# Weight parts split at a layer's end, on VectorE alone, and a layer that begins with the products of upper parts

## The chip, the cores and the metric

The kernel runs on one core of one Trainium2 chip. The metric is the device time of one execution in microseconds (us), from three runs of the kernel before: 2188.71, 2190.86 and 2193.92, median 2190.86. A separate execution was profiled; the rows in this document come from it.

Five engines run side by side, each in the order of its own instruction list, and wait for each other through semaphores: TensorE (PE, and PEld for its weight loads), VectorE (DVE), ScalarE (ACT), GpSimd (POOL) and SyncE (SP), which issues the large loads.

## The reference

The kernel computes two blocks in a row for 256 tokens of 1024 features. Block 1 (attention and 64 experts) takes the first half of the span and is not touched. Block 2 has two layers, each with a feed-forward part, a mixer and a second feed-forward part; every one of these six parts ends in a layer norm whose output is all that the next part reads:

```python
def swiglu(x, w_gate, w_up, w_down):
    return (jax.nn.silu(x @ w_gate) * (x @ w_up)) @ w_down

def second_block(x, mem, ln_g, ln_b, ...):
    alpha = DEEPNORM_ALPHA
    for l in range(DEPTH_2):                       # 2 layers
        x = layer_norm(alpha * x + 0.5 * swiglu(x, ffn_w_gate[l, 0], ffn_w_up[l, 0], ffn_w_down[l, 0]),
                       ln_g[l, 0], ln_b[l, 0])
        mem_kv = mem @ w_kv_mem[l]
        if l % N_MIXERS == 0:
            u = x @ w_in_conv[j]                   # convolution mixer
            tok = short_conv_mixer(u[..., :3 * D_TOK], conv_w[j])
        else:
            u = x @ w_in_mlstm[j]                  # mLSTM mixer
            tok = mlstm_mixer(...)
        xa = memory_cross_attention(u[..., -D_XA:], mem_kv)
        mix = jnp.concatenate([tok, xa], -1) @ w_out[l]
        x = layer_norm(alpha * x + mix, ln_g[l, 1], ln_b[l, 1])
        x = layer_norm(alpha * x + 0.5 * swiglu(x, ffn_w_gate[l, 1], ffn_w_up[l, 1], ffn_w_down[l, 1]),
                       ln_g[l, 2], ln_b[l, 2])
    return x
```

All weights and activations are float32, and the feed-forward width is 2816.

## The kernel before

**Products of two parts.** A float32 product is made of three faster ones. Each weight w is split into an upper part wh (a rounded copy, `wh`, made by ScalarE) and a lower part wl = w - wh (a subtraction); the activations likewise, as the pair of tiles `xT`. Then x @ w is taken as xh·wh + xh·wl + xl·wh, three matmuls into one PSUM bank (`mm3`, called by `xw`, L1144). A weight part is 1 MB: a load into one of the three raw slots of the ring (`wc` or `wr`, set by L1753), the copy wh on ScalarE, the subtraction wl on VectorE, or on GpSimd where `split` (L1100) is called with gp=True. The raw slot is free again after the subtraction. The two parts go to one of six pairs of tiles, taken in turn (four pairs from the mLSTM mixer on); a pair is free when the last matmul has read it.

**Blocks of tokens.** The 256 tokens are two blocks of 128, b = 0 and b = 1. At the end of a part of block 2 the sum of block 0 is finished first, three units of 12 matmuls before that of block 1 (the list at L1309, and the one in `mix_out`, L1368). Then `lnorm` (L1155) normalises the block: VectorE adds the residual (`h<-h,fd` or `h<-h,mo`), takes statistics, a few Newton steps on a column (L156 to L165), and two passes over each half (L1183, L1184); TensorE transposes each half (`lt`), ScalarE and VectorE make the two parts of `xT` from it. Nothing of the next part can be multiplied for a block until its `xT` is there.

**A part's beginning.** `ffn` (L1212) takes its width in chunks of 256 and five times 512. It begins with three weight tiles: the gate's and the up-projection's columns of the first chunk (`g0`, `u0`), and two halves of the second chunk's gate (`g1`), L1276 onward: all products of block 0 with g0, u0 and both halves of g1, then the same for block 1. g0 and both halves of g1 are split on GpSimd. The convolution mixer begins with three parts too (two on GpSimd or ScalarE and VectorE in turn), then a fourth on GpSimd; the mLSTM mixer with four on GpSimd, and one part of its w_out is also split there. The subtractions on VectorE are put by the scheduler behind the latest norm (`issue_after(self.after[1])`), unless marked early.

**What sets the order.** TensorE's order is the order of the program: large products are units, and the short steps of the norms and of other dependent chains go between them when the program's own clock says they are due, or when `wait` asks for their result. The other engines' order comes from a scheduler. SP's loads are in program order, each waiting for its raw slot.

Of the kernel before, what the change touches and what calls it, by code (L numbers as in the profile page):

```python
# [10 lines left out]
F32 = mybir.dt.float32  # L11
# [14 lines left out]
LN_EPS = 1e-5  # L26

# [45 lines left out]
class MixT:  # L73
    """Eight tiles of features in two places: the first n, and the others."""
# [13 lines left out]
class Kern:  # L88
# [29 lines left out]
    def slot(self, shape, name, pool=None):  # L118
        """One 8 KB slot of the weight ring."""
# [22 lines left out]
    def rms(self, pool, st, eps, name):  # L142
        """(mean of squares + eps) ^ -0.5 from the statistics of two halves."""
# [9 lines left out]
    def rsqrt(self, pool, out, hx, name):  # L153
        """(2 hx) ^ -0.5 of a few columns: a first guess from the bits, then Newton steps."""
# [83 lines left out]
    # ---------------------------------------------------------------- block 1: attention  # L238
    def phase_a(self):
# [41 lines left out]
        # u = rmsnorm(h) * gain, transposed, columns [meta | x]  # L281
# [33 lines left out]
        # z, features on partitions  # L315
# [20 lines left out]
        def gates():  # L336
            """log_a: log_sigmoid(a_low @ w_a2 + b_a), the 1/16 sits in the triangle; and its sums in a chunk."""
# [35 lines left out]
        def wide(n, src, scale, name):  # L373
            """(src * scale + eps) ^ -0.5 of a wide tile: exp(-ln/2) and a Newton step."""
# [9 lines left out]
        def keys():  # L384
            """MLA: the keys and values, and the rope of the shared keys, doubled on the partitions."""
# [31 lines left out]
        def queries():  # L417
            """MLA: the queries, and their rope, a pair of heads on the partitions, the other one zeroed."""
# [1412 lines left out]
```

## Time and profile before

| what | value |
|---|---|
| median of three runs (lowest, highest) | 2190.86 us (2188.71, 2193.92) |
| span of the profiled execution, first to last instruction (the page gives no other time of it) | 2193.5 us |
| mean granted TensorE clock of that execution | 0.974 of full speed |
| PE busy | 2009.8 us, 92% of the span |
| DVE busy | 956.9 us, 44% |
| ACT busy | 669.1 us, 31% |
| POOL busy | 123.4 us, 6%, 49 instructions |

Block 2 runs from about 1151 us to the end. A slice of the page in which PE shows 8 instead of 9 contains the passage from one part of block 2 to the next; PEclk is 9 (over 90% of full speed) in nearly all of them. The span is a sum of long stretches in which TensorE never waits and of six passages in which it does: from block 1 into the first feed-forward part (about 1151 us), into the convolution mixer (1357), the second (1454) and the third (1649) feed-forward part, the mLSTM mixer (1841) and the fourth feed-forward part (1960 to 2000).

### The profile page before, as it was taken

How to read it: one execution, taken by the hardware profiler on the slowest of the kernel's cores; microseconds unless marked ns; L12 is line 12 of the kernel's file. 1: busy time of each engine (PE TensorE's matmuls, PEld its weight loads, DVE VectorE, ACT ScalarE, POOL GpSimd, SP SyncE). 2: the span in 40 equal slices, each digit the busy share in tenths (PEclk: the TensorE clock that was granted, in tenths of full speed). 3: DMA queues.
4: the chain of work that ended last, by engine and by line, in shares of the span. 5: the costliest groups of instructions: out<-in, count | busy, mean ns of one | idle time of the engine just before them, and what ended most of it. 6: DMA issues, size and time to landing. Idle time of an engine off the chain costs nothing. (4 is left out here: it accounts for less than half of the span.)

```text
span 2193.5 us, 36714 instructions
## 1 busy us (share of the span) xinstructions
PE 2009.8 (92%) x15959; PEld 1407.1 (64%) x15959; DVE 956.9 (44%) x1439; ACT 669.1 (31%) x885; POOL 123.4 (6%) x49
## 2 busy tenths in 40 slices
PE   8989898988888898888888999999999999998998
PEld 7777453534444353535457887878887887887886
DVE  6553322222222222222236445765447445787455
ACT  6422111111111111111124433544334432843432
POOL 4000000000000000000011002020010002012000
PEclk9979999999999999999998999999999999999999
DMA  6458999999999999999996554546555543435552
GB/s 223 173 190 348 402 397 411 413 411 412 413 413 412 412 413 411 412 408 413 402 350 217 186 178 153 180 155 214 182 173 193 191 165 101 156 138 173 190 175 76
DMA packets 195943, 604.97 MB, mean 276 GB/s; under 512 B 9889, under 2 KB 26529, under 8 KB 195778
## 3 DMA queue, kind: packets, MB, share of 16 engines
q1 hardware_dynamic: 195554, 602.55, 72.4%
q8 instruction: 127, 2.08, 0.4%
q14 instruction: 38, 0.31, 0.0%
q10 hardware_dynamic: 224, 0.03, 0.0%
HBM read 601.49 MB, written 1.05 MB: 275 GB/s over the span
## 5 line engine op out<-in xcount | busy, mean ns | idle before, releaser
L975 DVE SCALAR_TENSOR_TENSOR h<-po,G,h 128x512 f32<-128x512 f32 x256 | 192.2, 751 | 366.4 <-PE po L116 346.1
L116 PE MATMUL pd<-ed,hT 128*32 128x512 f32 x1024 | 251.4, 644 | 47.3 <-DMA ed<-in_expert_w_down 36.8
L1118 DVE TENSOR_TENSOR wl<-wc,wh 128x2048 fp32r<-128x2048 f32 (+1 forms) x94 | 213.3, 2270 | 168.1 <-ACT wh L1114 168.0
L1114 ACT ACTIVATE wh<-wc 128x2048 fp32r<-128x2048 f32 (+2 forms) x114 | 212.8, 1871 | 239.6 <-PE fu L116 76.4
L116 PE MATMUL fg<-wh,xT 128*128 128x512 f32 (+1 forms) x768 | 234.4, 382 | 8.0 <-DVE xT L1124 8.0
L116 PE MATMUL po<-y,C 128*128 128x512 f32 x512 | 236.7, 605 | 3.8 <-ACT C L969 3.8
L116 PE MATMUL fd<-wh,hT 128*128 128x512 f32 x704 | 235.3, 402 | 0.0
L116 PE MATMUL fu<-wh,xT 128*128 128x512 f32 (+1 forms) x768 | 229.2, 377 | 0.0
L116 PEld LDWEIGHTS po<-y,C 128*128 128x128 f32 x512 | 91.8, 189 | 144.6 <-ACT y L964 72.6
L1118 POOL TENSOR_TENSOR wl<-wc,wh 128x2048 fp32r<-128x2048 f32 (+2 forms) x20 | 87.2, 4367 | 1669.6 <-PE po L116 1012.5
L1118 DVE TENSOR_TENSOR wl<-wr,wh 128x2048 fp32r<-128x2048 f32 x51 | 116.9, 2292 | 130.7 <-ACT wh L1114 130.7
L116 PE MATMUL pu<-eu,xg 128*32 128x128 f32 x4096 | 131.7, 274 | 41.2 <-DMA eu<-in_expert_w_up 40.7
L116 PEld LDWEIGHTS fg<-wh,xT 128*128 128x128 f32 x768 | 142.3, 191 | 37.6 <-DVE xT L1124 9.1
L116 PEld LDWEIGHTS fu<-wh,xT 128*128 128x128 f32 x768 | 140.8, 188 | 28.9
L949 DVE TENSOR_TENSOR hg<-sg,pu 128x128 f32<-128x128 f32 x64 | 18.5, 289 | 308.9 <-PE pu L116 308.9
L116 PEld LDWEIGHTS fd<-wh,hT 128*128 128x128 f32 x704 | 132.9, 189 | 30.8
L116 PEld LDWEIGHTS pd<-ed,hT 128*32 128x32 f32 x1024 | 51.2, 114 | 152.9 <-issue 97.9
L116 PEld LDWEIGHTS pu<-eu,xg 128*32 128x32 f32 x4096 | 109.8, 110 | 56.1 <-DMA eu<-in_expert_w_up 44.4
L116 PE MATMUL fg<-wl,xT 128*128 128x512 f32 (+1 forms) x384 | 145.6, 379 | 0.0
L116 PE MATMUL fu<-wl,xT 128*128 128x512 f32 (+1 forms) x384 | 144.6, 377 | 0.0
L116 PE MATMUL fd<-wl,hT 128*128 128x512 f32 x352 | 139.3, 396 | 0.0
L969 ACT COPY C<-pc 128x256 f32<-128x256 f32 x64 | 23.9, 373 | 371.0 <-PE pc L113 371.0
(497 smaller groups left out, 2545.9 us busy)
## 6 DMA issues: line engine op xcount, KB each, us to landing
eg<-in_expert_w_gate SPq DMA_DIRECT2D x128, 1024.0 KB, 18.4
eu<-in_expert_w_up SPq DMA_DIRECT2D x128, 1024.0 KB, 18.4
ed<-in_expert_w_down SPq DMA_DIRECT2D x128, 1024.0 KB, 18.4
wc<-in_ffn_w_gate SPq DMA_DIRECT2D x44, 1024.0 KB, 4.9
wc<-in_ffn_w_up SPq DMA_DIRECT2D x44, 1024.0 KB, 4.9
wr<-in_ffn_w_down SPq DMA_DIRECT2D x44, 1024.0 KB, 4.7
wc<-in_w_in_conv SPq DMA_DIRECT2D x10, 1024.0 KB, 5.0
wr<-in_w_out SPq DMA_DIRECT2D x8, 1024.0 KB, 4.8
```

The lines of the kernel that those rows point to most:

```text
L116: self.nc.tensor.matmul(out, lhsT, rhs, start=start, stop=stop, **kw)
L949: nc.vector.tensor_mul(hg, sg, pu[:, :P])
L969: nc.scalar.copy(C, p[:, :NX])
L975: nc.vector.scalar_tensor_tensor(self.h[:, b, cs], p, self.G[:, b, e:e + 1], self.h[:, b, cs], ALU.mult, ALU.add)
L1114: nc.scalar.activation(hi, raw, AF.Copy)
L1118: (nc.gpsimd if gp else nc.vector).tensor_sub(lo, raw, hi.bitcast(F32))
```

## The change

Seven edits, all in block 2.

- No subtraction of a weight part runs on GpSimd; the 21 that did are given to VectorE.
- The first three weight parts of a part of block 2 are loaded and split at the end of the part before it, just after that part's last weight has been split (`nxt()` in `ffn` and `mix_out`); for the mLSTM mixer these are its first two, kept out of the two pairs that close before it (keep).
- These subtractions are marked early (not behind a norm), except at the first and the last feed-forward part (defer=True), where only wh is made at first and the subtraction is made by `lower`, behind the norm of both blocks.
- `xw` takes a list of passes. A feed-forward part begins with the passes UPPER (xh·wh and xl·wh) of the three parts for block 0, then for block 1, then with LOWER (xh·wl) for block 0 and for block 1; the second half of g1 follows whole.
- The convolution mixer begins in the same way with its three parts.
- The flags that put some of these copies and subtractions late are dropped.
- Comments are removed.

```diff
+ALL, UPPER, LOWER = (0, 1, 2), (0, 2), (1,)
-    def split(self, raw, gp=False, late=False, early=False):
+    def split(self, raw, gp=False, late=False, early=False, keep=False, defer=False):
...
-            pool = self.pairs.pop(0)
+            pool = self.pairs.pop(next(a for a, x in enumerate(self.pairs) if not keep or x not in self.brief))
...
+        if defer:
+            return hi, lo, raw
...
+    def lower(self, w):
+
+        if len(w) == 3:
+            with self.tc.issue_after(self.after[1].ins):
+                self.nc.vector.tensor_sub(w[1], w[2], w[0].bitcast(F32))
+        return w[:2]
...
+    def xw(self, b, out, w, k0, passes=ALL):
...
-                x = [t[:, b, k] for t in self.xT]
-                self.mm3(out, x, (hi[:, k - k0, :], lo[:, k - k0, :]), k == 0, k == KD - 1)
-        self.unit(3 * kk * n / 2380, go)
+                xh, xl = (t[:, b, k] for t in self.xT)
+                for q in passes:
+                    x, y = ((xh, hi), (xh, lo), (xl, hi))[q]
+                    self.mm(out, x, y[:, k - k0, :], start=k == 0 and q == 0,
+                            stop=k == KD - 1 and q == passes[-1] and passes != UPPER)
+        self.unit(len(passes) * kk * n / 2380, go)
...
+    def ffn_first(self, l, j, defer=False):
+
+        wg, wu = (self.i[n][l, j] for n in ("ffn_w_gate_2", "ffn_w_up_2"))
+        src = [self.cols_w(wg, 0, 256)[0], self.cols_w(wu, 0, 256)[0], self.cols_w(wg, 256, 512)[0]]
+        return [self.split(x(), early=True, defer=defer) for x in src]
+
+    def conv_first(self):
+        w = self.i["w_in_conv_2"]
+        return [self.split(self.cols_w(w, 512 * c, 512)[h](), early=True) for c, h in ((4, 0), (4, 1), (3, 0))]
+
+    def mlstm_first(self):
+        w = self.i["w_in_mlstm_2"]
+        return [self.split(x(), early=True, keep=True) for x in self.cols_w(w, 3072, 264)]
...
-        g0 = self.split(self.cols_w(wg, *chunks[0])[0](), True)
-        u0 = self.split(self.cols_w(wu, *chunks[0])[0](), l + j == 0, early=True)
-        gl = self.cols_w(wg, *chunks[1])
-        g1 = [self.split(gl[0](), True)]
-        gu(0, "g", 0, 0, g0)
-        g1.append(self.split(gl[1](), True, l + j == 0))
-        gu(0, "u", 0, 0, u0)
-        for h in range(2):
-            gu(1, "g", h, 0, g1[h])
-        gu(0, "g", 0, 1, g0)
-        gu(0, "u", 0, 1, u0)
-        for h in range(2):
-            gu(1, "g", h, 1, g1[h])
+        lead = [(0, "g", 0), (0, "u", 0), (1, "g", 0)]
+        ws = self.first
+        for b in range(2):
+            for (c, which, h), w in zip(lead, ws):
+                gu(c, which, h, b, w, UPPER)
+        ws = [self.lower(w) for w in ws]
+        for b in range(2):
+            for (c, which, h), w in zip(lead, ws):
+                gu(c, which, h, b, w, LOWER)
+        w = self.split(self.cols_w(wg, *chunks[1])[1]())
+        for b in range(2):
+            gu(1, "g", 1, b, w)
...
                 w[q] = self.split(ws[q]())
+                if q == 3 and nxt:
+                    self.first = nxt()
...
-                w[part] = self.split(parts[part](), l == 1 and part == 2)
+                w[part] = self.split(parts[part]())
+                if part == 1:
+                    self.first = nxt()
...
-        ws = {}
-        for c, h in ((4, 0), (4, 1), (3, 0)):
-            ws[c, h] = self.split(self.cols_w(w, 512 * c, 512)[h](), h == 0, early=True)
-        for c, h, b in [(4, 0, 0), (4, 1, 0), (3, 0, 0), (3, 1, 0), (4, 0, 1), (4, 1, 1), (3, 0, 1), (3, 1, 1)] + \
-                [(c, h, b) for c in (2, 1) for h in range(2) for b in range(2)] + \
+        ws = dict(zip(((4, 0), (4, 1), (3, 0)), self.first))
+        for b in range(2):
+            for (c, h), x in list(ws.items()):
+                part(c, h, b, x, UPPER)
+        for b in range(2):
+            for (c, h), x in list(ws.items()):
+                part(c, h, b, x, LOWER)
+        for c, h, b in [(3, 1, 0), (3, 1, 1)] + [(c, h, b) for c in (2, 1) for h in range(2) for b in range(2)] + \
                 [(0, 0, 0), (0, 1, 0), (0, 0, 1), (0, 1, 1)]:
             if (c, h) not in ws:
-                ws[c, h] = self.split(self.cols_w(w, 512 * c, 512)[h](), (c, h) == (3, 1))
+                ws[c, h] = self.split(self.cols_w(w, 512 * c, 512)[h]())
...
-            ws[G[0], h] = self.split(self.cols_w(w, *G)[h](), True)
+            ws[G[0], h] = self.first[h]
...
-        part(*Q[0], 0, 0, True)
-        p0 = part(*Q[0], 1, 0, True)
+        part(*Q[0], 0, 0)
+        p0 = part(*Q[0], 1, 0)
...
+                self.brief = [self.pair(more) for _ in range(2)]
+                self.first = self.ffn_first(0, 0, defer=True)
+                self.ffn(0, 0, 0, lambda: self.conv_first())
+                self.conv_mixer(0, lambda: self.ffn_first(0, 1))
+                self.ffn(0, 1, 2, lambda: self.ffn_first(1, 0))
+                self.ffn(1, 0, 0, lambda: self.mlstm_first())
+            self.brief = []
+            self.mlstm_mixer(1, lambda: self.ffn_first(1, 1, defer=True))
+            self.ffn(1, 1, 2, None)
```

Where it moves instructions, by the order of the built programs. **First, TensorE at the beginning of the second feed-forward part**, around the transposes `lt` of block 1's norm. xT_9588 and xT_9589 are the upper and lower part of the activations, `fu` the up-projection's and `fg` the gate's products. Before, they stand behind all 24 products of g0 and all 24 of u0 for block 0 and are followed by those of g1 for block 0:

```order
L116 MATMUL fu_11717<-wh_11674,xT_9588 128x256
L116 MATMUL fu_11717<-wl_11675,xT_9588 128x256
L116 MATMUL fu_11717<-wh_11674,xT_9589 128x256
L113 MATMUL lt_11742<-cst_63,h 128x128 x4
L116 MATMUL fg_11753<-wh_11680,xT_9588 128x512
L116 MATMUL fg_11753<-wl_11681,xT_9588 128x512
L116 MATMUL fg_11753<-wh_11680,xT_9589 128x512
```

Now:

```order
L117 MATMUL fg_11718<-wh_11564,xT_9588 128x512
L117 MATMUL fg_11718<-wh_11564,xT_9589 128x512
L114 MATMUL lt_11727<-cst_63,h 128x128 x4
L114 MATMUL lt_11734<-cst_63,h 128x128 x4
L117 MATMUL fg_11741<-wh_11552,xT_9588 128x256
L117 MATMUL fg_11741<-wh_11552,xT_9589 128x256
```

Ahead of these transposes now stand 40 products of block 0: 16 of g0, 16 of u0 (256 columns each) and 8 of the first half of g1 (512 columns); before, 48 of 256 columns, with 24 of 512 to follow before block 1's. Behind them come block 1's products at once; the products with wl of both blocks come after those.

**Second, VectorE at the beginning of the mLSTM mixer**, in the norm of block 1 (`mvf`, `vf`, `rf`, `f101nt` are its columns; 128x1536 is a weight part of the first queries). Before:

```order
L1166 BN_AGGR mvf_14216<-stf_14211 128x2
L1173 TENSOR_SCALAR vf_14218<-mvf_14216 128x1
L1183 SCALAR_TENSOR_TENSOR h<-h,mvf_14216,lng_12947 128x512
L156 TENSOR_SCALAR rf_14219<-vf_14218 128x1
L1183 SCALAR_TENSOR_TENSOR h<-h,mvf_14216,lng_12947 128x512
L157 TENSOR_SCALAR rf_14219<-rf_14219 128x1
L1556 TENSOR_TENSOR ga<-mu_14268,bg 128x8
L161 SCALAR_TENSOR_TENSOR f101nt<-rf_14219,vf_14218 128x1
```

Now:

```order
L1182 BN_AGGR mvf_14228<-stf_14223 128x2
L1123 TENSOR_TENSOR wl_14299<-wc_14296,wh_14298 128x1536
L1189 TENSOR_SCALAR vf_14230<-mvf_14228 128x1
L1199 SCALAR_TENSOR_TENSOR h<-h,mvf_14228,lng_12965 128x512
L157 TENSOR_SCALAR rf_14231<-vf_14230 128x1
L1199 SCALAR_TENSOR_TENSOR h<-h,mvf_14228,lng_12965 128x512
L158 TENSOR_SCALAR rf_14231<-rf_14231 128x1
L1594 TENSOR_TENSOR ga<-mu_14268,bg 128x8
L162 SCALAR_TENSOR_TENSOR f101nt<-rf_14231,vf_14230 128x1
L1123 TENSOR_TENSOR wl_14318<-wc_14315,wh_14317 128x1536
```

The two subtractions that GpSimd made now stand inside the norm of block 1.

**Third, VectorE at the end of the norm of block 1, ahead of the fourth feed-forward part** (`h<-h,rm,lnb` is its last pass). Before:

```order
L1184 SCALAR_TENSOR_TENSOR h<-h,rm_15566,lnb_14238 128x512 x2
L1245 TENSOR_TENSOR hs_15674<-sg_15632,fu_15640 128x256
L1124 TENSOR_TENSOR xT_9589<-lt_15665,xT_9588 128x512
L1124 TENSOR_TENSOR xT_9589<-lt_15689,xT_9588 128x512
L1124 TENSOR_TENSOR hT_15673<-ht_15708,hT_15672 128x256
L1118 TENSOR_TENSOR wl_15804<-wc_15801,wh_15803 128x2048
```

Now:

```order
L1200 SCALAR_TENSOR_TENSOR h<-h,rm_15581,lnb_14250 128x512 x2
L1136 TENSOR_TENSOR xT_9589<-lt_15647,xT_9588 128x512
L1136 TENSOR_TENSOR xT_9589<-lt_15654,xT_9588 128x512
L1130 TENSOR_TENSOR wl_15476<-wc_15473,wh_15475 128x2048
L1130 TENSOR_TENSOR wl_15481<-wc_15478,wh_15480 128x2048
L1130 TENSOR_TENSOR wl_15486<-wc_15483,wh_15485 128x2048
L1277 TENSOR_TENSOR hs_15727<-sg_15715,fu_15621 128x256
```

The three deferred subtractions follow the norm; until they are made, the three raw slots stay taken. The first feed-forward part has the same order.

## Rows read from the trace of the kernel before

**Rows 1.** Who waited for whom, PE, 1140 to 2190 us: total, times, longest

```profile
PE lt L113 <- DVE h L1184: 10.5, 7, 2.3
PE fg L116 <- DVE xT L1124: 8.0, 5, 1.8
PE lt L113 <- DVE h L1181: 7.6, 1, 7.6
PE mo L116 <- DVE xT L1124: 2.3, 1, 2.3
```

**Rows 2.** Windows: stretch, us, busy PE PEld DVE ACT POOL, PEclk, DMA

```profile
1158.60:1168.20 9.60, 7.74 (x34) 7.23 (x35) 4.67 (x14) 3.01 (x4) 4.57 (x1) 0.50 0.60 178
...
1358.30:1362.90 4.60, 4.50 (x15) 3.33 (x16) 4.50 (x9) 1.03 (x2) 0.36 (x2) 0.67 0.68 228
...
1843.20:1848.40 5.20, 5.17 (x19) 4.13 (x20) 5.20 (x4) 0.60 (x1) 3.42 (x2) 0.67 0.60 176
1962.90:1967.00 4.10, 4.09 (x13) 3.22 (x14) 4.10 (x4) 0.63 (x1) 0.00 (x0) 0.64 0.75 254
1984.10:1989.10 5.00, 4.98 (x16) 3.75 (x17) 5.00 (x2) 0.60 (x1) 4.33 (x1) 0.66 0.01 2
```

**Rows 3.** Groups of instructions on POOL, 1090 to 2190 us

```profile
L1118 POOL TENSOR_TENSOR wl<-wc,wh 128x2048 fp32r<-128x2048 f32 (+2 forms) x20 | 87.2, 4367 | 1669.6 <-PE po L116 1012.5 <-ACT wh L1114 642.9 <-DMA wc<-in_ffn_w_gate 14.2
```

**Rows 4.** Timeline, DVE, into the second feed-forward part: start, us, what

```profile
1449.85 5.75 DVE L1184 SCALAR_TENSOR_TENSOR h<-h,rm,lnb 128x512 f32<-128x512 f32 x2
...
1457.44 0.67 DVE L1163 SCALAR_TENSOR_TENSOR h<-h,mo 128x512 f32<-128x512 f32 x1
...
1462.56 1.42 DVE L1184 SCALAR_TENSOR_TENSOR h<-h,rm,lnb 128x512 f32<-128x512 f32 x2
...
1464.87 0.69 DVE L1124 TENSOR_TENSOR xT<-lt,xT 128x512 fp32r<-128x512 f32 x1 [0.56 <-ACT xT L1123]
```

**Rows 5.** Timeline, POOL, the same passage

```profile
1449.96 5.09 POOL L1118 TENSOR_TENSOR wl<-wc,wh 128x2048 fp32r<-128x2048 f32 x1 [3.76 <-ACT wh L1114]
```

**Rows 6.** Chain that ended last, the same passage: start, us, what

```profile
1460.92 2.84 PE fu L116 x24
1463.76 0.44 PE lt L113 x4
```

**Rows 7.** Timeline, DVE, from block 1 into block 2

```profile
1145.76 2.09 DVE L1170 SCALAR_TENSOR_TENSOR vfin<-mvfin 128x1 f32<-128x1 f32 x1
...
1149.41 2.93 DVE L161 SCALAR_TENSOR_TENSOR fin0nt<-rfin,vfin 128x1 f32<-128x1 f32 x1
1152.37 4.42 DVE L165 SCALAR_TENSOR_TENSOR rfin<-fin0nt,rfin 128x1 f32<-128x1 f32 x1
1156.82 0.22 DVE L161 SCALAR_TENSOR_TENSOR fin0nt<-rfin,vfin 128x1 f32<-128x1 f32 x1
...
1160.97 1.41 DVE L1181 SCALAR_TENSOR_TENSOR h<-h,rfin,fing 128x512 f32<-128x512 f32 x2
```

**Rows 8.** Timeline, POOL, the same passage

```profile
1143.30 13.47 POOL L1118 TENSOR_TENSOR wl<-wc,wh 128x2048 fp32r<-128x2048 f32 x3 [1012.53 <-PE po L116]
```

**Rows 9.** Timeline, PE, the same passage

```profile
1158.63 1.94 PE L113 MATMUL lt<-cst,h 128*128 128x128 f32 x8 [7.61 <-DVE h L1181]
```

**Rows 10.** Timeline, DVE, into the mLSTM mixer

```profile
1842.42 4.65 DVE L1184 SCALAR_TENSOR_TENSOR h<-h,rf,lnb 128x512 f32<-128x512 f32 x2
```

**Rows 11.** Timeline, DVE, at the end of the mLSTM mixer

```profile
1953.46 4.58 DVE L164 TENSOR_TENSOR ml11nt<-ml11nt,mvv 128x2 f32<-128x2 f32 x1
```

**Rows 12.** Groups of instructions on DVE by shape, 1090 to 2190 us

```profile
L1118 DVE TENSOR_TENSOR wl<-wc,wh 128x2048 fp32r<-128x2048 f32 x88 | 202.8, 2305 | 166.1 <-ACT wh L1114 166.0
```

**Rows 13.** Page, DMA issues: count, KB each, median us to landing

```profile
eg<-in_expert_w_gate SPq DMA_DIRECT2D x128, 1024.0 KB, 18.4
...
wc<-in_ffn_w_gate SPq DMA_DIRECT2D x44, 1024.0 KB, 4.9
```

**Rows 14.** Windows, the lead of the first feed-forward part

```profile
1168.20:1189.40 21.20, 21.20 (x133) 18.89 (x133) 11.63 (x10) 11.96 (x11) 0.00 (x0) 0.99 0.60 212
```

More of the change, by code (lines that the diff above doesn't have):

```diff
@@ L1142, in rows_w @@
         return [lambda k0=k0: self.load([P, 2, D], v[:, k0:k0 + 2, :], "wr") for k0 in range(0, nk, 2)]
-    def xw(self, b, out, w, k0):
-        hi, lo = w
+    def xw(self, b, out, w, k0, passes=ALL):
+        hi, lo = w[:2]
         kk, n = hi.shape[1:]
@@ L1209, in ln_params, with ffn @@
         return g, b
-    def ffn(self, l, j, ln, last=False):
+    def ffn_first(self, l, j, defer=False):
[8 more added lines that the diff above has]
+        return [self.split(x(), early=True, keep=True) for x in self.cols_w(w, 3072, 264)]
+    def ffn(self, l, j, ln, nxt):
         nc, i = self.nc, self.i
+        last = nxt is None
         wg, wu, wd = (i[n][l, j] for n in ("ffn_w_gate_2", "ffn_w_up_2", "ffn_w_down_2"))
@@ L1257, in ffn, with gu @@
         self.pg = {}
-        def gu(c, which, h, b, w):
+        def gu(c, which, h, b, w, passes=ALL):
             n = chunks[c][1]
@@ L1264, in gu @@
             self.wait(self.ln[b])
-            if h == 0:
+            if h == 0 and 0 in passes:
                 ps[c, b] = self.ps("f" + which)
-            self.xw(b, ps[c, b][:, :n], w, h * kk)
-            if (h + 1) * kk == KD:
+            self.xw(b, ps[c, b][:, :n], w, h * kk, passes)
+            if (h + 1) * kk == KD and 1 in passes:
                 if which == "g":
@@ L1366, in cross, with mix_out @@
         self.split_t(tT[0][:, b, 6:8], tT[1][:, b, 6:8], pv)
-    def mix_out(self, l, tT, g, bt, needs):
+    def mix_out(self, l, tT, g, bt, needs, nxt):
         parts = self.rows_w(self.i["w_out_2"][l], 0, KD)
@@ L1389, in mix_out, with conv_mixer @@
                 self.start_ln(b, acc[b], self.alpha, LN_EPS, g, bt, f"m{l}{b}", self.sp)
-    def conv_mixer(self, l):
+    def conv_mixer(self, l, nxt):
         nc, i = self.nc, self.i
@@ L1452, in conv_mixer, with part @@
         xa, ends, ps = [None, None], {}, {}
-        def part(c, h, b, wc):
+        def part(c, h, b, wc, passes=ALL):
             self.wait(self.ln[b])
-            if h == 0:
+            if h == 0 and 0 in passes:
                 ps[c, b] = self.ps("cu")
-            self.xw(b, ps[c, b], wc, 4 * h)
-            if h == 1:
+            self.xw(b, ps[c, b], wc, 4 * h, passes)
+            if h == 1 and 1 in passes:
                 if c < 4:
@@ L1475, in needs, with mlstm_mixer @@
             return xa[b] if part == 3 else ends[1 if part == 2 else 0, b]
-        self.mix_out(l, tT, g, bt, needs)
+        self.mix_out(l, tT, g, bt, needs, nxt)
         ctx.close()
-    def mlstm_mixer(self, l):
+    def mlstm_mixer(self, l, nxt):
         nc, i = self.nc, self.i
@@ L1657, in mlstm_mixer, with part @@
         ps, ws, xa, ce = {}, {}, [None, None], {}
-        def part(c0, n, h, b, pool=False):
+        def part(c0, n, h, b):
             if (c0, h) not in ws:
-                ws[c0, h] = self.split(self.cols_w(w, c0, n)[h](), pool)
+                ws[c0, h] = self.split(self.cols_w(w, c0, n)[h]())
             hi, lo = ws[c0, h]
@@ L1718, in mlstm_mixer @@
             oc.append(self.chain(out_end(b, *hs)))
-        self.mix_out(l, tT, g, bt, lambda part, b: xa[b] if part == 3 else oc[b])
+        self.mix_out(l, tT, g, bt, lambda part, b: xa[b] if part == 3 else oc[b], nxt)
         for c in (gt0, gt1):
@@ L1735, in block2 @@
             with ExitStack() as more:
-                for _ in range(2):
-                    self.pair(more)
-                self.ffn(0, 0, 0)
-                self.conv_mixer(0)
-                self.ffn(0, 1, 2)
-                self.ffn(1, 0, 0)
-            self.mlstm_mixer(1)
-            self.ffn(1, 1, 2, last=True)
+                self.brief = [self.pair(more) for _ in range(2)]
[7 more added lines that the diff above has]
+            self.ffn(1, 1, 2, None)
         ctx.close()
```

1 line of the change is left out of this document (added).

## The prediction

> **What bounds the kernel now.** I read the page's engine shares first: TensorE is busy for 92% of the span and VectorE for 44%, so nothing but TensorE's own work sets most of the end, and a change that leaves the number of products as it is can only win or lose time in which TensorE waits or is slowed. So the waits of TensorE in block 2 come next [rows 1]: transposes for the last pass of a norm 10.5 us, products for the second part of xT 8.0 and 2.3, transposes for the last norm of block 1 7.6; together 28.4 us, all at the six passages. Then windows around the passages, for the clock [rows 2]. A granted clock of 0.50 is the lower of its two levels (1.2 of 2.4 GHz) for the whole stretch, 0.67 is the lower one for two thirds of it; each of these stretches follows an idle time of TensorE. What they cost: 7.74 us of busy time at 0.50 is 3.9 us; 4.6 x 0.33, 5.2 x 0.33, 4.1 x 0.36 and 5.0 x 0.34 are 1.5, 1.7, 1.5 and 1.7; in all 10.3 us. The passages thus hold 28.4 + 10.3 = 38.7 us, and that is all there is to win.
>
> Why TensorE waits is read from the timelines of VectorE and GpSimd laid side by side. Into the second feed-forward part the last pass of block 0's norm took 5.75 us for two instructions, and the same two for block 1 took 1.42 [rows 4]; the first pair began 0.11 us before a GpSimd subtraction of 5.09 us began, and ended 0.55 us after it [rows 5]. At the entry of block 2 two instructions on one column took 2.93 and 4.42 us, where an instruction of the same kind took 0.22 right behind [rows 7], and GpSimd was in one row of three subtractions from 1143.30 to 1156.77 [rows 8]; with a third (2.09 us, so three against some 0.2 each) 8.85 us were lost there. Into the mLSTM mixer a last pass took 4.65 [rows 10], near its end a step on two columns 4.58 [rows 11]. So the late norms are VectorE instructions that stand still while GpSimd subtracts.
>
> **What the change costs and gives, part by part.**
>
> *No subtraction on GpSimd.* It removes the 20 subtractions of the row (87.2 us of GpSimd, 4.37 each) and one more whose tile has another name [rows 3]. VectorE gets 21 at up to 2.305 us [rows 12], at most 48 us, on an engine idle for over half of the span. They are no cost where they lie behind TensorE's long runs, which is where a part's end puts them (its last weight has been split, the products of the last units are still to come). If that cover is missing, each is 2.3 us of a norm; that is counted below where the order shows one inside a norm. The stalls go: the norm of block 0 into a feed-forward part is 5.75 - 1.42 = 4.3 us earlier, more than TensorE waited for it at any one time (2.3 at the longest, [rows 1]); the entry of block 2 is 8.85 us earlier.
>
> *Loads and copies at the end of the part before.* As many loads and copies as before, earlier in SP's and ScalarE's order. SP issues in order and each load waits for a raw slot; an early subtraction frees the slot at once, so I take nothing. At the first and the last feed-forward part the subtraction is deferred behind the norm of both blocks and three raw slots stay taken until then. A 1 MB load lands in 4.9 us in one group of this queue's loads and in 18.4 us in another [rows 13]. The second half of g1 is loaded when the first of them comes free: 8.1 us for block 1's norm (below) and 2.3 for a subtraction, then 4.9 for the load and some 2.3 for the copy (an estimate, by the subtraction of the same tile): 17.6 us from the start. TensorE meanwhile has 5.7 us of upper products for each block (below) and half as much of lower ones, 17.0 in all. So I take it 0.6 us late; by 18.4 it would be 13.5 later still, and that end stays for a rival.
>
> *Upper products first.* The count of products stays. What changes is the cover for block 1's norm. From the start of block 1's residual (1457.44) to the end of its first lower xT (1464.87 + 0.69) it takes 8.1 us [rows 4]. Before, TensorE had all products of block 0 with g0, u0 and both halves of g1 for that time: 48 of 256 columns and 24 of 512. 24 of 256 take 2.84 us [rows 6], so that is 11.4. Now 40 stand there, 32 of 256 columns (3.8 us) and 8 of 512 (1.9): 5.7 us, plus 0.44 for the transposes [rows 6]. So a wait of 8.1 - 5.7 - 0.4 = 2.0 us comes in where block 0's wait goes. The convolution mixer has 24 of 512 columns there, 5.7 too. This is the wait that is late next, at passages two to four: 2.0 each, 6.0.
>
> *The other passages.* Entry of block 2: without the stalls block 1's last pass ends at 1160.97 + 1.41 - 8.85 = 1153.5 [rows 7], and with its transposes and 0.69 for xT [rows 4] block 0 could start at 1154.2 at the earliest. TensorE was free 7.61 us before 1158.63, at 1151.0, and has 1.9 us of transposes [rows 9], to 1152.9: 1.3 us left, and I add 1.1 for block 1 behind the shorter cover and 0.6 for the late load: 3.0. mLSTM mixer: the order puts both subtractions of the first queries (1536 of 2048 columns, so 1.73 us each by the row of 2.305) inside block 1's norm, 3.5 us between nothing and all of it late; I take 1.6, with 2.1 for a 2.3 us subtraction that stands in block 0's norm, 3.7 in all. End of the mLSTM mixer and fourth feed-forward part: the floor is 2.0 as elsewhere; the upper end is the longest wait of each kind in [rows 1], 2.3 for mo, 2.3 for the transposes of each block and 1.8 for xT, 8.7. I take 4.3, nearer the floor, as the stall of [rows 11] goes, but not the floor, as three subtractions of w_out are new on VectorE there.
>
> *The clock.* Waits of 1.5 to 2.3 us stood before a slower stretch at some passages; at the second and third feed-forward part none such shows in [rows 2]. With shorter waits I take two of six, 1.7 us each: 3.4.
>
> *Sum.* Left: 3.0 + 6.0 + 3.7 + 4.3 + 3.4 = 20.4. Gain 38.7 - 20.4 = 18.3 us. The profiled span 2193.5 becomes 2175.2; the median of the runs was 2.6 us under that span, which gives 2172.6. Bounds: waits halved (8.5) and no slower stretch gives a gain of 30.2 (2160.7); waits doubled and as much of slower clock as before (34 + 10.3) gives a loss of 5.6 (2196.5).
>
> **The rivals.** (0.2% or 4.4 us is taken as what a measurement here tells from no change.)
>
> *Block 1's norm costs more than I take.* For it: cover falls from 11.4 to 5.7 us at every passage. If the wait is 3.0 and each passage has its slower stretch (6 x 1.7 = 10.2), 18 + 10.2 are left, the gain is 10.5: 2180. Against it: the 8.1 us are measured in a norm without a stall, and the shorter cover is the one that I count. Chance 0.2.
>
> *VectorE becomes the bound of the lead.* In the first feed-forward part's lead of 21.2 us it was busy 11.63 [rows 14]; four subtractions more make 20.9 of 21.2. If each of six leads is late by one subtraction (13.8), the gain is 4.5: 2186, on the border of no change. Against it: three of the four are made before the lead in four of the six parts, and the row of 2.305 already has 88 of these without a wait of TensorE for them in [rows 1]. Chance 0.06.
>
> The Trainium skill's page "Perfetto Trace Analysis" (section "Optimizing Scalar/DVE Operations") would rather have it the other way round: a saturated VectorE is a reason to give work to ScalarE or even GpSimd. By that the lead of [rows 14] would be late as in this rival, and the time its 2186. The same paragraph says that the two share a read port, so that moving work between them may not help; the trace agrees with that half, with 4.3 us lost by one pair of instructions beside a 5.09 us subtraction [rows 4, 5].
>
> *Raw slots, slower.* At the first and the last feed-forward part the three held slots make the loads behind them come in a row. If they land in 18.4 us instead of 4.9 [rows 13], TensorE is late by 13.5 at both, 27 - 18.3 = 8.7 us slower: 2199.6. It decides from a landing of some 14 us (2 x 9.2 eats the gain). For it: 18.4 is the median of 128 loads in this kernel. Against it: the 44 of the other row, on the same queue, have 4.9. Chance 0.05.
>
> *The stalls are not GpSimd's doing.* Then the norms stay slow (38.7 stays) and the shorter cover adds about 1 us at each of five passages: 2196. Against it: two places where rows of both engines stand side by side [rows 4, 5, 7, 8], and GpSimd busy for 3.42 and 4.33 us in two of the slower stretches [rows 2]. Chance 0.03.
>
> *Everything hides.* Gain over 27 us, 2164 or less: no slower stretch, and norms of block 1 quicker than 8.1 us. Chance 0.07.
>
> **How the numbers follow.** My forecast 0.59, with 2166 to 2179; exposed norm 0.2; VectorE 0.06; slots 0.05; no stall 0.03; all hidden 0.07. Faster by over 0.2% is below 2186.5: the forecast, the exposed norm, the hidden case and half of the VectorE case, less a little for the tails: 0.86. Within 0.2%: 0.07; slower: 0.07. The range 2160 to 2185 leaves out the two slower cases, part of VectorE's and the end of the hidden one.
>
> **What would show it.** No subtraction in GpSimd's rows, and every last pass of a norm in block 2 at about 0.7 us each (before some took two to four times that). TensorE's wait of 7.6 us gone, its waits for the last pass of block 0's norm gone, and in their place waits of 1 to 3 us for the second block's xT behind 40 upper products. Fewer than five slower stretches. Wrong would be: long waits of TensorE for wl at the beginning of a part (VectorE the bound), loads at the first or the last feed-forward part that land in over 10 us with TensorE waiting for wh, or instructions on columns that still take over 2 us with GpSimd idle.

## The result, and the profile after

The changed kernel takes 2170.9 us (median of 4 runs, 2170.06 to 2172.11); the kernel before, run beside it, 2189.78. The ratio is 0.9905, 95% interval 0.9891 to 0.9919: 18.9 us faster. Measured again in the experiments below it took 2172.13 where the kernel before had 2193.98 on the same chip, ratio 0.9893 (0.9876 to 0.9911), 21.9 us. The forecast was 2172.6 us, 18.3 us faster.

The profiled execution has a span of 2169.7 us, 23.8 less than that of before. Runs differ by some us in block 1, which the change doesn't touch: TensorE ends its products with wkv between 1150.7 and 1154.6 us in the traces of this document. (Where spans, or "the last norm of block 1", are meant, block 1 and block 2 are the two blocks of the network; otherwise, of a norm, a transpose or an xT, block 0 and block 1 are the two blocks of tokens.) So block 2 is also told by itself below, from the time at which TensorE is free of them (the start of the first transposes `lt` less the idle time ahead) to the end of the span. Before it is 2193.5 - (1158.63 - 7.61) = 1042.5 us [rows 9], after 2169.7 - 1151.09 = 1018.6.

First the waits of TensorE from 1140 us on, as in [rows 1] (total, times, longest):

```profile
PE fg L117 <- DVE xT L1136: 4.6, 8, 1.7
PE my L114 <- DVE hn L1683: 1.5, 1, 1.5
PE mu L117 <- DVE wl L1123: 1.1, 1, 1.1
PE fg L117 <- ACT xT L1135: 1.0, 4, 0.3
PE lt L114 <- DVE h L1200: 1.0, 1, 1.0
```

The 10.5 us for a norm's last pass are 1.0 now, the 7.6 us at the entry of block 2 are gone, the 8.0 for xT are 4.6. The 1.0 that is left for a last pass stands ahead of the mLSTM mixer. All waits together fell from 30.9 to 12.8 us. Of the five slower stretches [rows 2] one is left, right at the entry (stretch, busy times by engine, granted clock):

```profile
1155.00:1159.00 4.00, 4.00 (x23) 4.00 (x22) 0.00 (x0) 0.00 (x0) 0.00 (x0) 0.57 0.41 144
```

It costs 4.0 x 0.43 = 1.7 us, where the five cost 10.3. Next the page's engines of after, GpSimd last (busy, share, instructions):

```profile
PE 2003.4 (92%) x15959; PEld 1402.0 (65%) x15959; DVE 955.4 (44%) x1460; ACT 668.3 (31%) x885; POOL 31.3 (1%) x28
```

VectorE's groups by shape (busy us, mean ns), of after:

```profile
L1123 DVE TENSOR_TENSOR wl<-wc,wh 128x2048 fp32r<-128x2048 f32 x98 | 223.8, 2291 | 177.7 <-ACT wh L1117 177.6
L1200 DVE SCALAR_TENSOR_TENSOR h<-h,rf,lnb 128x512 f32<-128x512 f32 x16 | 11.3, 748 | 0.3
L1200 DVE SCALAR_TENSOR_TENSOR h<-h,rm,lnb 128x512 f32<-128x512 f32 x8 | 5.7, 750 | 0.1
```

and the last two groups as they stood before:

```profile
L1184 DVE SCALAR_TENSOR_TENSOR h<-h,rf,lnb 128x512 f32<-128x512 f32 x16 | 23.2, 1492 | 0.3
L1184 DVE SCALAR_TENSOR_TENSOR h<-h,rm,lnb 128x512 f32<-128x512 f32 x8 | 14.3, 1828 | 0.1
```

GpSimd lost 21 instructions and 92 us. VectorE got those 21 and is busy for 955.4 us where it was 956.9, though they are some 45 us of work (17 of 2048 columns at 2.29 us, two of 1536 at 1.75, two of 1056 at 1.26). The mean of 4.37 us in [rows 3] mixes the same three widths: the sixteen of 2048 columns took 4.69 us each on GpSimd. The 24 last passes alone gave back 16 x 0.744 + 8 x 1.078 = 20.5 us. So a busy time in these rows holds the time in which an instruction stands still, and VectorE paid for GpSimd's subtractions without making them.

Into the second feed-forward part, VectorE's last passes and lower parts of xT, which answer to [rows 4]:

```profile
1440.88 1.42 DVE L1200 SCALAR_TENSOR_TENSOR h<-h,rm,lnb 128x512 f32<-128x512 f32 x2
...
1450.38 1.42 DVE L1200 SCALAR_TENSOR_TENSOR h<-h,rm,lnb 128x512 f32<-128x512 f32 x2
...
1453.26 1.29 DVE L1136 TENSOR_TENSOR xT<-lt,xT 128x512 fp32r<-128x512 f32 x2 [1.46 <-ACT xT L1135]
```

and TensorE there (in brackets the idle time ahead and who ended it):

```profile
1447.31 1.10 PE L117 MATMUL fg<-wh,xT 128*128 128x256 f32 x7 [0.59 <-DVE xT L1136]
...
1452.00 1.03 PE L114 MATMUL lt<-cst,h 128*128 128x128 f32 x8
1453.28 0.39 PE L117 MATMUL fg<-wh,xT 128*128 128x256 f32 x1 [0.25 <-ACT xT L1135]
1454.01 2.04 PE L117 MATMUL fg<-wh,xT 128*128 128x256 f32 x15 [0.34 <-DVE xT L1136]
```

Block 0's last pass takes 1.42 us instead of 5.75, and its transposes wait for nothing. Block 1's xT is late by 0.25 and 0.34 us behind the 40 upper products, and block 0's second half by 0.59: 1.2 us of idle time. The first product after a wait takes 0.39 us by itself, where one more in a row takes some 0.12 ((2.04 - 0.39) / 14), so that by this estimate each short wait also costs some 0.27 us that count as busy. Block 1's norm itself is in time: its last pass ends at 1451.80, and TensorE begins the transposes at 1452.00 without a wait. Late is the step behind them, the two parts of xT on ScalarE and VectorE, since block 1's products stand right behind both halves of its transposes.

The entry of block 2, TensorE and then VectorE:

```profile
1151.09 1.04 PE L114 MATMUL lt<-cst,h 128*128 128x128 f32 x8
1152.38 0.39 PE L117 MATMUL fg<-wh,xT 128*128 128x256 f32 x1 [0.25 <-ACT xT L1135]
1154.44 2.68 PE L117 MATMUL fg<-wh,xT 128*128 128x256 f32 x15 [1.67 <-DVE xT L1136]
...
1175.97 0.50 PE L117 MATMUL fg<-wl,xT 128*128 128x512 f32 x1 [0.47 <-DVE wl L1123]
```

```profile
1152.37 1.42 DVE L1197 SCALAR_TENSOR_TENSOR h<-h,rfin,fing 128x512 f32<-128x512 f32 x2
1153.70 1.28 DVE L1136 TENSOR_TENSOR xT<-lt,xT 128x512 fp32r<-128x512 f32 x2
```

The transposes no longer wait; block 0's xT does, for 1.67 us, because VectorE makes block 1's last pass (1152.37) before the lower part of block 0's xT (1153.70). The 0.47 at 1175.97 is the second half of g1, whose load had to wait for a raw slot.

### The profile page after: what moved, and what is told of

It is laid out like the page before. It is cut to its first block, busy times and chain, and to the rows that moved or that the text cites. A ratio compares the mean times of both kernels' runs of the same rounds, so it can differ in the third digit from the quotient of the medians.

```text
span 2169.7 us, 36697 instructions
## 1 busy us (share of the span) xinstructions
PE 2003.4 (92%) x15959; PEld 1402.0 (65%) x15959; DVE 955.4 (44%) x1460; ACT 668.3 (31%) x885; POOL 31.3 (1%) x28
## 4 chain that ended last, share of the span: by engine, by line
PE 58%; DMA 23%; DVE 4%; SPq 1%; ACT 1%; issue 1%; DVEq 0%; ACTq 0%
DMA ed<-in_expert_w_down 12%; PE fu L117 11%; PE fg L117 11%; PE fd L117 11%; DMA eu<-in_expert_w_up 10%; PE pd L117 5%; PE po L117 4%; PE cu L117 2%; PE mu L117 2%; PE ps L117 2%; PE pg L117 2%; PE pu L117 2%; PE mo L117 2%; SPq L140 1%; PE ht L114 1%
## 5 line engine op out<-in xcount | busy, mean ns | idle before, releaser
L1123 DVE TENSOR_TENSOR wl<-wc,wh 128x2048 fp32r<-128x2048 f32 (+2 forms) x108 | 240.3, 2231 | 181.7 <-ACT wh L1117 181.5
L117 PE MATMUL fg<-wh,xT 128*128 128x512 f32 (+1 forms) x768 | 222.1, 381 | 5.6 <-DVE xT L1136 4.6
L117 PE MATMUL fu<-wh,xT 128*128 128x512 f32 (+1 forms) x768 | 221.8, 378 | 0.0
L117 PEld LDWEIGHTS fg<-wh,xT 128*128 128x128 f32 x768 | 136.4, 189 | 36.0 <-DVE xT L1136 6.2
L117 PEld LDWEIGHTS pg<-eg,xg 128*32 128x32 f32 x4096 | 107.8, 110 | 44.3 <-issue 39.7
L117 PE MATMUL fu<-wl,xT 128*128 128x512 f32 (+1 forms) x384 | 135.4, 376 | 0.0
L1117 ACT ACTIVATE wh<-wr 128x2048 fp32r<-128x2048 f32 x52 | 99.6, 1915 | 105.3 <-PE fd L117 56.9
```

What stands on the lines that cost most here:

```text
L117: self.nc.tensor.matmul(out, lhsT, rhs, start=start, stop=stop, **kw)
L1117: nc.scalar.activation(hi, raw, AF.Copy)
L1123: (nc.gpsimd if gp else nc.vector).tensor_sub(lo, raw, hi.bitcast(F32))
```

## The experiments

The theory: what cost the time was VectorE standing still beside a GpSimd instruction that reads SBUF, where that was in a norm or in a chain of small steps. The rivals: that it is the time at which these subtractions stand; that the new order of products is a part of the gain; that the raw slots are. The first runs (engine only to nothing deferred) stood beside a before of 2193.88 us, the others beside one of 2193.98 on another chip.

| run | median us | ratio to before (95%) | block 2, us |
|---|---|---|---|
| before | 2193.9 | | 1042.5 |
| the change (again) | 2172.13 | 0.9893 (0.9876 to 0.9911) | 1018.6 (1017.3) |
| engine only | 2178.97 | 0.9927 (0.9907 to 0.9947) | 1025.6 |
| all passes in one | 2166.87 | 0.9865 (0.9845 to 0.9886) | 1013.8 |
| early ones on GpSimd | 2173.78 | 0.9901 (0.9881 to 0.9920) | 1021.9 |
| nothing deferred | 2180.90 | 0.9936 (0.9918 to 0.9955) | 1027.7 |
| GpSimd reads | 2187.68 | 0.9964 (0.9948 to 0.9980) | 1034.1 |
| GpSimd writes | 2172.37 | 0.9899 (0.9882 to 0.9917) | 1018.9 |
| combined | 2162.83 | 0.9855 (0.9838 to 0.9872) | 1010.6 |

**The engine alone**, on the kernel before (`self.pairs` is there in block 2 only):

```diff
-            (nc.gpsimd if gp else nc.vector).tensor_sub(lo, raw, hi.bitcast(F32))
+            (nc.gpsimd if gp and not self.pairs else nc.vector).tensor_sub(lo, raw, hi.bitcast(F32))
```

> The kernel before, with nothing changed but the engine: the 21 subtractions of block 2 that GpSimd made are made by VectorE, unordered to the norms, in the old place of the program. Theory (what cost time was VectorE standing still beside a GpSimd subtraction): the 4.4 us stalls are gone, but where the built order puts a subtraction into a norm (three at the entry of block 2, one ahead of xT of block 0 at the next three parts, four at the mLSTM mixer) 1.7 to 2.3 us each come back: some 10 to 16 us faster than before, about 2178, with the waits of the transposes for block 0's norm gone at passages two to four and the entry still 6 us or more. Rival (it is the time at which these subtractions stand, not their engine): at most 5 us faster, 2185 or more.

Measured: 15 us faster than before, and 17 of the change's 24 us in block 2. TensorE's longest waits, and at the entry of block 2 the subtractions on VectorE:

```profile
PE lt L113 <- DVE h L1184: 8.4, 6, 3.9
PE lt L113 <- DVE h L1181: 5.0, 1, 5.0
```

```profile
1147.11 2.24 DVE L1118 TENSOR_TENSOR wl<-wc,wh 128x2048 fp32r<-128x2048 f32 x1
...
1150.70 2.28 DVE L1118 TENSOR_TENSOR wl<-wc,wh 128x2048 fp32r<-128x2048 f32 x1
...
1153.08 2.23 DVE L1118 TENSOR_TENSOR wl<-wc,wh 128x2048 fp32r<-128x2048 f32 x1
1156.59 1.41 DVE L1181 SCALAR_TENSOR_TENSOR h<-h,rfin,fing 128x512 f32<-128x512 f32 x2
```

As the theory has it, also in the remainder: three subtractions of 6.75 us stand in the last norm of block 1 in place of stalls of 8.85 [rows 7], and the entry still costs 5.0. The waits of the norm's last pass didn't quite go at the middle passages (0.92 to 1.16 us each), which the expectation had wrong. The longest, 3.9, stands ahead of the fourth feed-forward part, where two subtractions (2.24 and 2.28 us) lie inside block 1's norm; before, the wait there was 0.15. The rival falls: the old time on the new engine gives most of the gain.

**All passes in one** at the three middle parts:

```diff
+        early = len(ws[0]) == 2
         for b in range(2):
             for (c, which, h), w in zip(lead, ws):
-                gu(c, which, h, b, w, UPPER)
+                gu(c, which, h, b, w, ALL if early else UPPER)
         ws = [self.lower(w) for w in ws]
-        for b in range(2):
+        for b in range(0 if early else 2):
...
             for (c, h), x in list(ws.items()):
-                part(c, h, b, x, UPPER)
-        for b in range(2):
-            for (c, h), x in list(ws.items()):
-                part(c, h, b, x, LOWER)
+                part(c, h, b, x, ALL)
```

> The changed kernel, but where the first three parts are split early (convolution mixer, second and third feed-forward part) all three passes of block 0 are made before block 1's, with no separate lower passes; the first and the last feed-forward part keep the new order. Theory (upper first shortens the cover for block 1's norm from 8.5 to 5.7 us and wins nothing where wl is there early): the waits for block 1's xT of 0.25 + 0.34 us at these three passages go, 1 to 3 us faster than the changed kernel, 2168 to 2170. Rival (upper first is a part of the gain): slower than the changed kernel by 3 us or more, with TensorE waiting for wl at the beginning of these parts.

Measured: 4.8 us less than the change in block 2. The waits for xT:

```profile
PE fg L117 <- DVE xT L1136: 2.7, 4, 1.7
```

Four of eight are left, those of the first and the last feed-forward part; at the second and third TensorE does not wait at all, and into the convolution mixer once, 0.41 us. That is 3.2 us of idle time; the rest of the 4.8 fits the slow first products behind waits, of which there are nine fewer (an estimate: 9 x 0.27 = 2.4 us), but was not taken apart. It is more than the 1 to 3 us expected. So the upper products first are no part of the gain where the weights are split early; they cost there. The two halves of block 1's transposes, which stood together at 1452.00, now stand apart, with products of block 0 between them:

```profile
1453.11 0.60 PE L114 MATMUL lt<-cst,h 128*128 128x128 f32 x4
...
1456.36 0.60 PE L114 MATMUL lt<-cst,h 128*128 128x128 f32 x4
```

ScalarE and VectorE make the parts of xT under these products. The run changes this place and the number of products ahead of block 1's together; which of the two counts is not shown.

**The early ones on GpSimd** (the first three parts where they are not deferred, with `gp`):

```diff
-        return [self.split(x(), early=True, defer=defer) for x in src]
+        return [self.split(x(), not defer, early=True, defer=defer) for x in src]
```

and `True` likewise in `conv_first` and `mlstm_first`.

> The changed kernel, with the 11 subtractions that are made early (three of the convolution mixer, three each of the second and third feed-forward part, two of the mLSTM mixer) on GpSimd again, the rest on VectorE. In the changed kernel the three stand 17, 12 and 5 us ahead of the residual of block 0's norm into the third feed-forward part, so 4.4 us each on GpSimd would be over before it. Theory (a GpSimd subtraction costs only where it lies beside a norm): within 2 us of the changed kernel, 2170 to 2173. Rival (GpSimd as such is the cost): stalls of 2 to 5 us come back in VectorE's norms, with waits of TensorE for the norm's last pass and stretches at the lower clock, 2175 to 2180.

Measured: 1.6 us slower than the change by the medians (the intervals overlap), 3.3 in block 2, more than the 2 expected. GpSimd at the last of the three ahead of the third feed-forward part and ahead of the mLSTM mixer, then VectorE at the latter:

```profile
1623.62 4.65 POOL L1123 TENSOR_TENSOR wl<-wc,wh 128x2048 fp32r<-128x2048 f32 x1 [1.40 <-ACT wh L1117]
...
1828.16 2.46 POOL L1123 TENSOR_TENSOR wl<-wc,wh 128x1056 fp32r<-128x1056 f32 x1 [20.73 <-DVE f100nt L162]
```

```profile
1828.17 2.46 DVE L166 SCALAR_TENSOR_TENSOR rf<-f100nt,rf 128x1 f32<-128x1 f32 x1
1830.66 0.22 DVE L162 SCALAR_TENSOR_TENSOR f100nt<-rf,vf 128x1 f32<-128x1 f32 x1
```

Where the three end ahead of the norm, the passage has the waits of the changed kernel to 0.01 us. The one place that got slower has a subtraction inside the norm: an instruction on one column, 0.16 us elsewhere, takes 2.46, just as long as the subtraction beside it (VectorE itself makes that one in 1.26 in the changed kernel), and TensorE waits 2.2 us where it waited 1.0, with a slower stretch of 1.7 behind. So a subtraction on GpSimd shows no cost ahead of a norm, and does inside one.

**Nothing deferred** (`defer=True` dropped at both places):

```diff
-                self.first = self.ffn_first(0, 0, defer=True)
+                self.first = self.ffn_first(0, 0)
...
-            self.mlstm_mixer(1, lambda: self.ffn_first(1, 1, defer=True))
+            self.mlstm_mixer(1, lambda: self.ffn_first(1, 1))
```

> The changed kernel without the deferring: the first three subtractions of the first and the last feed-forward part are made at once as at the others. The built order puts three of them inside block 1's last norm. Theory (a subtraction inside a norm costs what it takes): the entry of block 2 is some 5 to 7 us later, the last passage is about as it is, 2174 to 2179. Rival (raw slots that are held are what the first and the last part wait for): TensorE's waits for wl at the first part (0.5 us) go and the time falls by 1 to 2 us, 2169 to 2170.

Measured: 8.8 us slower than the change by the medians, 9.1 in block 2; 2180.90 lies above the expected 2174 to 2179:

```profile
PE lt L114 <- DVE h L1197: 5.0, 1, 5.0
PE fg L117 <- DVE xT L1136: 4.9, 8, 2.1
PE lt L114 <- DVE h L1200: 3.8, 3, 1.7
```

The 5.0 of the run with the engine alone are back at the entry, which is some 6.6 us dearer than in the change (4.7 of waits, 1.9 of slower clock), as expected; and the fourth feed-forward part, where no cost was expected, has two waits of 1.7 and 1.1. So without the deferring, the early splitting and the new order together give no more than the engine alone (1027.7 against 1025.6). The rival of the raw slots falls: freeing them gained the 0.5 us at the most.

**The changed kernel again**, to measure the next three beside it:

> The changed kernel itself, beside the next three on one chip, as the measure for them and for the four before. Theory and rival alike: within 3 us of its first measurement, 2168 to 2174.

2172.13 us, as expected. Its waits at the entry are those of the first trace to 0.01 us, but for the second half of g1 (0.32 for 0.47), and there is no stretch at the lower clock in block 2 at all; without it block 2 is 1.3 us shorter.

**GpSimd reads, GpSimd writes.** Work that nobody needs, at five norms of block 0:

```diff
         nc.vector.bn_aggr(mv, st)
+        if bt is not None and b == 0 and not last:
+            z = self.scr.rearrange("p (a b) -> p a b", b=P)
+            nc.gpsimd.tensor_copy(self.scr[:, 0:2], mv)
+            i4 = self.c("ident").unsqueeze(1).to_broadcast([P, 3, P])
+            for _ in range(5):
+                nc.gpsimd.tensor_sub(z, i4, i4)
```

and in the second kernel, in place of the last three lines:

```diff
+            for _ in range(11):
+                nc.gpsimd.memset(self.scr, 0.0)
```

> The changed kernel with work for GpSimd that nobody needs: at five norms of block 0 (into the convolution mixer, the second and third feed-forward part, the mLSTM mixer and the fourth feed-forward part) five subtractions of two constants in SBUF, 384 columns each, some 4 us in all, released by the norm's mean. Theory (VectorE stands still beside a GpSimd instruction that reads SBUF): the norm's passes and its steps on columns take about 4 us longer in all, TensorE waits for the last pass again at these five passages, 2 to 4 us each, some with a stretch at the lower clock: 10 to 25 us slower than the changed kernel, 2181 to 2196. Rival (the stalls had another cause, for instance the late copies on ScalarE): within 2 us of the changed kernel.

> As the run before, but with eleven memsets of the same 384 columns, about as long in all, in place of the five subtractions, so that GpSimd only writes. Theory (it is the reading that stops VectorE): within 2 us of the changed kernel, no norm instruction over 1.6 us for a pair. Rival (any GpSimd instruction on SBUF stops VectorE): as slow as the run before, 10 to 25 us over the changed kernel.

Measured: the reads cost 15.5 us, the writes nothing. Into the second feed-forward part, VectorE beside the reads and what GpSimd did; TensorE's waits over block 2 last:

```profile
1442.45 0.14 DVE L157 TENSOR_SCALAR rm<-vm 128x1 int32<-128x1 int32 x1
1442.52 1.25 DVE L1205 SCALAR_TENSOR_TENSOR h<-h,mvm,lng 128x512 f32<-128x512 f32 x1
...
1443.86 0.60 DVE L162 SCALAR_TENSOR_TENSOR m00nt<-rm,vm 128x1 f32<-128x1 f32 x1
...
1446.50 1.87 DVE L1206 SCALAR_TENSOR_TENSOR h<-h,rm,lnb 128x512 f32<-128x512 f32 x2
```

```profile
1442.06 5.10 POOL L1188 TENSOR_TENSOR scr<-cst 128x384 f32<-128x384 f32 x5
```

```profile
PE lt L114 <- DVE h L1206: 12.1, 5, 3.7
```

The same place beside the writes, VectorE and then GpSimd (nine of its eleven memsets, as the stretch begins behind the first two):

```profile
1439.22 0.74 DVE L1204 SCALAR_TENSOR_TENSOR h<-h,mvm,lng 128x512 f32<-128x512 f32 x1
...
1440.06 0.22 DVE L162 SCALAR_TENSOR_TENSOR m00nt<-rm,vm 128x1 f32<-128x1 f32 x1
...
1441.41 1.41 DVE L1205 SCALAR_TENSOR_TENSOR h<-h,rm,lnb 128x512 f32<-128x512 f32 x2
```

```profile
1439.71 4.23 POOL L1187 MEMSET scr<- 128x384 f32 x9
```

Beside the reads the passes (1.25 for 0.74, 1.87 for 1.41) and a step with two operands on columns (0.60 for 0.22) take some 0.4 to 0.5 us more each; the step with one operand in SBUF (L157, 0.14) takes what it always does; beside the writes nothing changes. TensorE waits 11.1 us more for the last pass than in the changed kernel (12.1 against 1.0), and the lower clock costs 4.5 more (6.2 against 1.7, in windows of 1 us): the 15.5. This puts the cause of before back, in the changed kernel, and the run with the writes has the same tile and the same order with other GpSimd instructions. The Trainium skill says it in these terms on the page "SBUF — State Buffer" (section "Who interferes with whom"): a VectorE instruction with two inputs in SBUF contends with a GpSimd instruction that reads SBUF, not with one that only writes. These two runs agree, with 1.25 against 0.74 us for the same pass.

**Combined**: all passes in one as above, and two subtractions of w_out put behind the product hn*so at the end of the mLSTM mixer. In the changed kernel three of them stand in the chain of small steps that this product ends:

```profile
1938.37 2.28 DVE L1123 TENSOR_TENSOR wl<-wr,wh 128x2048 fp32r<-128x2048 f32 x1
...
1941.24 2.29 DVE L1123 TENSOR_TENSOR wl<-wr,wh 128x2048 fp32r<-128x2048 f32 x1
...
1944.60 2.28 DVE L1123 TENSOR_TENSOR wl<-wr,wh 128x2048 fp32r<-128x2048 f32 x1
...
1948.17 0.96 DVE L1683 TENSOR_TENSOR hn<-hn,so 128x768 f32<-128x768 f32 x1
```

```diff
+            if behind is not None:
+                order.enter_context(self.tc.issue_after(behind.ins))
             (nc.gpsimd if gp else nc.vector).tensor_sub(lo, raw, hi.bitcast(F32))
...
-            nc.vector.tensor_mul(hf, hf, so[:, b, :])
+            self.hm = nc.vector.tensor_mul(hf, hf, so[:, b, :])
...
-                w[part] = self.split(parts[part]())
+                w[part] = self.split(parts[part](), behind=self.hm if l == 1 and part < 2 else None)
```

> The run with all passes in one at the three middle parts, and two of the three subtractions of w_out at the end of the mLSTM mixer are put behind the product hn*so of block 1, whose chain of small steps they stand in now. Theory (a 2.3 us subtraction within a chain that TensorE waits for costs what it delays): TensorE's wait of 1.46 us for hn goes, 1 to 1.5 us faster than that run, 5 to 7 us faster than the changed kernel, 2163 to 2167 where the changed kernel has 2171. Rival (the parts of w_out are then late themselves): TensorE waits for wl of w_out, no faster or up to 2 us slower than that run.

Measured: 2162.83 us, 31 us under before and 9.3 under the change beside it; its interval (0.9838 to 0.9872) lies below the change's (0.9876 to 0.9911). That is just under the expected 2163 to 2167. In block 2 it is 6.7 us under the second trace of the change (neither has a slower stretch), 1010.6 against 1017.3, as expected; block 1 is another 3.0 us shorter in this trace, which the edit doesn't touch. Against the run with all passes in one block 2 is 3.2 us shorter, of which 1.7 is that run's slower stretch at the entry; the 1.5 left are what was expected. VectorE there now:

```profile
1931.38 2.28 DVE L1125 TENSOR_TENSOR wl<-wr,wh 128x2048 fp32r<-128x2048 f32 x1
...
1936.55 0.95 DVE L1683 TENSOR_TENSOR hn<-hn,so 128x768 f32<-128x768 f32 x1
1937.42 2.28 DVE L1125 TENSOR_TENSOR wl<-wr,wh 128x2048 fp32r<-128x2048 f32 x1
```

The product begins 6.1 us after that of block 0 (1936.55 against 1930.43) instead of 10.8 (1948.17 against 1937.42), TensorE's wait of 1.46 us for it is gone, and no wait for a part of w_out came in.

## Why the prediction was right, and where its sum was not

*The stalls.* Right, and it is the step that decides: the 24 last passes went from 1.5 and 1.8 us to 0.75, the entry's transposes wait no more, and the run with the engine alone has 17 of the 24 us. The reads and writes on GpSimd show the cause itself.

*21 subtractions on VectorE for nothing.* Right in the sum, since its busy time didn't grow, and right that each one inside a norm costs its time: the run with the engine alone and that with nothing deferred show it at the entry (5.0 us of wait), and the combined run at the end of the mLSTM mixer (1.46). VectorE as the bound of the lead fell with that: TensorE waits 0.47 us in the first lead of [rows 14].

*Block 1's norm as the next wait.* Right in place, wrong in its path and too large. 2.0 us were counted at each of passages two to four, and 1.2 were measured as idle time (0.6 or less of it for block 1), with some 0.8 more as slow first products; the sign of 1 to 3 us for block 1's xT was missed. The sum lets its 8.1 us begin with block 0's products. In the trace of after, block 1's residual begins at 1443.83, 1.6 us before the first of these products (1445.40), while TensorE still makes block 1's last sums. The 8.1 themselves start from the residual's second half; its first half began 1.3 us earlier, at 1456.12. So the norm is done when TensorE reaches the transposes, and only the parts of xT behind them are waited for. The run with all passes in one leaves none of this wait.

*The raw slots.* 0.47 us were measured for the 0.6 counted at the entry, and the loads land in 4.9 us still, as in [rows 13]. But the sum's path was wrong and the match is luck: it ends with the copy wh, and that was done at 1173.59, ahead of its first product at 1175.02. TensorE waited for wl, whose subtraction the sum leaves out:

```profile
1173.62 2.29 DVE L1123 TENSOR_TENSOR wl<-wc,wh 128x2048 fp32r<-128x2048 f32 x1 [1.79 <-ACT wh L1117]
```

*The other passages.* The entry's 3.0 us were 2.98, though not term by term: 1.9 for block 0's xT where 1.3 was counted, 0.6 for block 1 where 1.1 was. The mLSTM mixer and the passage after it were mis-sized: 3.7 and 4.3 were counted, 2.5 and 2.1 measured. At the mixer the 1.6 for the first queries was 1.54 (1.08 and 0.46); the 2.1 for block 0's norm was 0.97, because the subtraction in it is not one of 2048 columns and 2.3 us:

```profile
1827.44 1.26 DVE L1123 TENSOR_TENSOR wl<-wc,wh 128x1056 fp32r<-128x1056 f32 x1
```

At the passage after it the waits were 1.46 for hn, behind the subtractions of w_out, and twice 0.34 for xT. *The clock*: one stretch of 1.7 where two were counted.

*The sum.* In the profile 23.8 us were won, not 18.3; the terms that were too large are those of block 1's norm, the last two passages and the clock. That the forecast time (2172.6) came out within 2 us of the measured one is in part chance: 2.6 us were taken off as the distance of the profiled span from the runs' median, and after the change the median lies 1.2 above the span. The profiled execution of before was a long one among its first runs: a run's time lies some 1.8 us above its span (2171.46 against 2169.7 after), so by this estimate it took 2195.3, where the median then was 2190.86 (later medians were 2193.9). These two errors, 5.5 and 3.8 us, go against each other.

## What to carry to other kernels

When a small VectorE instruction takes microseconds in one place and a fraction in another, lay GpSimd's timeline beside it: a GpSimd instruction that reads SBUF stops VectorE's instructions with two SBUF operands for as long as it lasts (2.46 us beside one of 2.46), and work given to GpSimd is free only where VectorE has nothing that someone waits for. Moving such work in time (ahead of the chain) was worth as much here as moving it to VectorE, and on VectorE it still costs its length inside a chain. An order made for a late operand (upper products first) costs where that operand is early: ask at each place which operand is last. Whether it pays where wl is late, at the first and the last feed-forward part, no run here shows.

## What the runs showed of the hardware

Two executions of the same kernel with the same waits for xT at the entry of block 2 (1.67 and 1.68 us ahead of the same products) differ in the clock behind them: one has a stretch at 0.57, 1.7 us lost, the other none. Of the seven traces with this wait five have the stretch. So a slower stretch of this length can't be put down to a wait of that length alone, and comparisons of single profiles are uncertain by 1.7 us here. Why one execution has it stays open.

A GpSimd subtraction of 384 columns took 1.0 us and a memset of as many 0.42; the subtraction of 2048 columns 4.69 where VectorE takes 2.29. VectorE's standing still is counted as busy time of the instruction that stands.
